# Weight lows split on chip in every pass of a Strassen layer, with reloads one tile at a time

## The chip, the cores and the metric

The kernel runs on one core of a Trainium2 chip. The metric is the device time of one execution in microseconds (us); lower is better. The engines are TensorE (PE in the profile, its weight loads PEld), VectorE (DVE), ScalarE (ACT), GpSimd (POOL) and SyncE (SP). DMAs are issued from SP's and POOL's queues here.

## The reference

One layer of a hybrid network is applied to a prompt of 2048 tokens and to a decoding batch of 64 tokens, model width 1024, all in float32. Cut to what matters (`B, T` are batch and tokens):

```python
h = rms_norm(x, g_pre)
vA, bA, cA, zA, q, f, iv, zB, gA, gB = split_cols(h @ w_in)     # w_in: 1024 x 10240
u = cA * vA
conv = causal_conv3(concat(conv_hist, u), conv_w)               # three taps
yA = (silu(zA) * bA * conv) @ w_a_out
fg = lb + (1 - lb) * sigmoid(f);  logf = log(fg);  kk = 1 - fg
S_new, o = hgrn2_scan(S0, silu(q) * QK_SCALE, kk, iv, logf)     # gated linear attention, 8 heads, chunks of 64
o = o * rsqrt(mean(o * o) + EPS) * g_onorm
yB = (o * silu(zB)) @ w_b_out
out = (sigmoid(gA) * yA + sigmoid(gB) * yB) @ w_o
x = x + rms_norm(out, g_post)
gate = sigmoid(rms_norm(x, g_ple) @ w_ple_gate)
x = x + (p @ w_ple_proj) * gate
```

The outputs are the new x of both token sets, the last two columns of u and the attention states.

## The kernel before

**Passes.** The 2112 tokens are cut into three blocks of 768, 704 and 640 columns (`SIZES`). Each block is one pass over all weights, so every weight is read from device memory three times. Activations lie with features on the partitions. A pass runs the gates gA and gB (`gates`), the heads (`path_b`: two weight groups a head, and the attention), path A (`path_a`), then the merges W_A, W_B and the output W_O, then two norms (`final_norm`) and the gate W_G. Work of neighbouring passes is interleaved: the norm of one pass runs as side work during the gates of the next, and `final_gate` of one pass runs at a later place.

**Precision.** A float32 operand x is split into hi, x rounded to the reduced format float32r (a cast on ScalarE), and lo = x - hi (a subtraction on VectorE). `split` (L195) is this pair. A product is hi·hi + hi·lo + lo·hi, three matmuls.

**Strassen.** Weights come in column pairs (i1, i2). With two halves of the contraction this makes four weight blocks of 128 x 4 x 128 numbers, 256 KB each: A11, A21, A22, A12. Seven products with A11, A12, A22 ("plain" blocks, taken as they are) and the sums S1 to S4 replace eight. One product of one pair is 4 x 3 = 12 matmuls. `sgroup` (L363) does the seven products of one pair in the order of `PRODUCTS`: A11, S3, S1, S2, A12, A22, S4. `combined` (L301) gives it the weights. A pass has 40 such pairs before its merges: 8 of the gates, 16 of the heads, 16 of path A. In the first pass two of them (the last of gB, and FF/QQ of head 0) are done by `plain_group` (L427) without Strassen.

`in_turn` (L486) does W_A, W_B and W_O, and W_G in the last pass, in another order: each of the seven products of `IN_TURN` (A11, A12, S2, S3, A22, S1, S4) for all four pairs, then the next. I call one of these seven a turn; it has four products, g = 0 to 3.

**Where hi and lo of weights come from.** In the first pass `combined` loads the four raw blocks, forms the sums on VectorE, splits all seven, and stores to device memory the sums (`keep_sum`, L288) and all seven lows (`split_w`, L221, stores when it is given a key that it has not seen). In later passes `kept_w` (L294) loads the raw block or the stored sum, casts hi on ScalarE, and *loads* the low: `split_w` finds the key in `lows`, takes a buffer from `low_tile` (L211) and issues the load on SP's queue. Such a group has 14 loads of 256 KB.

**Buffers.** `raw` has 5 tiles, `hi` 5, `lo` 4, and `s` (sums in the first pass) 3. `low_tile` counts its calls and gives an s tile at three of seven calls and a lo tile at the others. A DMA waits on its queue until the tile's last reader is done, and everything behind it on that queue waits too.

**Side work.** `hook()` is called after each product and runs the next piece of other work from a list written out by hand: steps of the attention (`head_attn`), of the norm, of the next pass's operands. `prepare_sums` (L327) computes sums S1 to S4 of W_A, W_B, W_O and W_G ahead of their use, in pieces. A piece is one sum on VectorE (L359), its split (L196), and two stores from POOL's queue (L341, L345); the raw blocks come by POOL as well (L336). In the first pass, the eight pairs of W_A and W_B are prepared during the heads, 4 pieces a head, and the four pairs of W_O during path A (`side`, L1384).

**Reloads.** Tensors spilled earlier come back through POOL's queue in the merge stage: gA tiles, attention outputs ("o") and gB tiles by `loads` (L1136), four tiles after certain turns; in the last pass the rows "h2" of the pass before, by `rows_again` (L1231), four tiles at a time and then four splits. `paced` (L253) makes such a DMA wait for the matmul issued last before it.

**Order.** The Tile framework places instructions by priority and keeps that order on each engine; `tc.high_priority()` moves weight loads, casts and splits forward, `issue_after` and `behind_all` queue side work behind named instructions.

Of the kernel before, what the change touches and what calls it, by code (L numbers as in the profile page):

```python
# [18 lines left out]
P = 128  # L19
D = 1024  # L20
KB = D // P
# [67 lines left out]
def hybrid_step(  # L89
# [31 lines left out]
    def nm(s):  # L121
        uid[0] += 1
        return f"{s}_{uid[0]}"
# [86 lines left out]

    def low_tile():  # L211

        turn[0] += 1
        if turn[0] % 7 in (1, 3, 5):
            return sum_tile(F32R)
        return wp.tile([P, 4, P], F32R, tag="lo", name=nm("lo"))
# [4 lines left out]
    def split_w(raw, key=None, queue=SP):  # L221

        hi = wp.tile([P, 4, P], F32R, tag="hi", name=nm("hi"), bufs=5)
        if key in lows:
            lo = low_tile()
            A.copy(hi, raw)  # L226
            SP.dma_start(lo.bitcast(F32), lows[key])
            return hi, lo
        lo = wp.tile([P, 4, P], F32R, tag="lo", name=nm("lo"))
        split(raw, hi, lo)  # L230
        if key is not None:
            lows[key] = dram.tile([P, 4, P], F32, tag=f"lo{key}", name=nm("low"), bufs=1)
            queue.dma_start(lows[key], lo.bitcast(F32))
        return hi, lo
# [59 lines left out]
    def kept_w(i1, i2, name, anew=False):  # L294

        keys = dict(A11=(i1, 0), A12=(i1, 1), A22=(i2, 1))
        if name in keys:
            return split_w(load_raw(w_blk[keys[name]]), None if anew else keys[name])
        return split_w(load_raw(sums[i1][name]), (i1, name))

    def combined(i1, i2, first):  # L301

        queue = SP if first else G
        with tc.high_priority():
            if not first and i1 in sums:
                return {n: kept_w(i1, i2, n) for _, n, _, _, _ in PRODUCTS}
            a11, a21, a22, a12 = (load_raw(w_blk[i, h]) for i, h in ((i1, 0), (i2, 0), (i2, 1), (i1, 1)))
            out = dict(A11=split_w(a11, (i1, 0), queue))
# [10 lines left out]
            out["A12"] = split_w(a12, (i1, 1), queue)  # L319
            out["A22"] = split_w(a22, (i2, 1), queue)  # L320
# [165 lines left out]
    def in_turn(stages, operand):  # L486
# [10 lines left out]
        for i, (st, n) in enumerate(todo):  # L497
# [44 lines left out]
            yield st["idx"], n  # L542
# [497 lines left out]
    def path_b(bl, hc, first, kept, fills, hs, extra, phases):  # L1040
# [13 lines left out]
        for hd in range(NH):  # L1054
# [6 lines left out]
            for i, before in enumerate((wait, 0, wait, 1)):  # L1061
                hooks.extend([None] * before)
                hooks.extend(partial(step_of, g, extra if i in phases else None) for g in attn)
                hooks.extend([None] * (NPART - len(attn)))
# [56 lines left out]
    def merge_in_turn(a, kept, mg):  # L1121
# [14 lines left out]
        def loads(idx, n):  # L1136
# [9 lines left out]
            if kind is not None:  # L1146
                tiles.extend(reload(kept[kind, j], n >= 0) for j in range(len(tiles), len(tiles) + KH))
# [6 lines left out]
    def out_in_turn(mg, xo, acc):  # L1154
# [14 lines left out]
        return dict(idx=W_O, raw=mg, sink=sink, anew=())  # L1169
# [61 lines left out]
    def rows_again(kept, h2):  # L1231

        for _ in range(2):
            for j in range(len(h2), len(h2) + KH):
                hi, lo = (rt(wide(kept["h2", j]), F32R) for _ in range(2))
                paced(G.dma_start(lo.bitcast(F32), kept["h2", j]))
                h2.append((hi, lo))
            yield
            for hi, lo in h2[-KH:]:
                split(lo.bitcast(F32), hi, lo)  # L1240
            yield
# [127 lines left out]
    for bi, bl in enumerate(blocks):  # L1369
# [4 lines left out]
        in_heads = pairs_of(W_A) + pairs_of(W_B) if first else late if middle else None  # L1374
        in_path = pairs_of(W_O) if first else pairs_of(W_G) if bl["last"] else None
# [8 lines left out]
        def side(rows, sums_):  # L1384
            for j in range(KB):
# [4 lines left out]
                elif sums_ is not None:  # L1390
                    at = (2, 9) if j < KB - 2 else (2, 6, 10)
# [10 lines left out]
        stages.append(out_in_turn(mg, xo, acc))  # L1402
# [10 lines left out]
        loads(W_A, -1)  # L1413
        for idx, n in in_turn(stages, a_first):
# [3 lines left out]
            if idx == W_O and n in (0, 2, 3, 5):  # L1418
                next(again)
            if (idx, n) == (W_O, 4):  # L1420
# [73 lines left out]
```

## Time and profile before

| | |
|---|---|
| median of three runs | 2576.79 us (2576.73 to 2579.15) |
| the profiled execution | 2578.22 us |
| its span, first to last instruction | 2576.4 us |
| granted PE clock, mean | 0.998 |
| PE busy | 2546.8 us (99%) |
| DVE, ACT busy | 1730.9 us (67%), 1589.4 us (62%) |
| DMA | 775.87 MB, 301 GB/s over the span |

Where the stages lie in the profile, from the timeline (start to end, us): first pass, start and plain groups to 78; gates, heads and path A 78 to 703; merges 704 to 887. Second pass, gates 887 to 986 and, after the first pass's W_G (986 to 1054), heads and path A 1054 to 1563; merges 1563 to 1728. Third pass, gates, heads and path A 1728 to 2284; merges 2284 to 2442, with W_O from about 2384; then W_G of the second pass to 2506 and of the third from 2521 to the end.

How to read it: one execution, recorded by the hardware. `L380` is line 380 of the kernel before. `lo<-low` is a load of a stored low into a lo tile, `s<-low` the same into an s tile, `low<-lo` a store; `pg` and `pa` are PSUM tiles of products and of the attention; `r` is a tile of the large ring buffer. A row of waits such as `PE pa L614 <- DVE r L634: 0.3, 1, 0.3` says that PE was idle before instructions of L614 that write a pa tile for 0.3 us in total, once, the longest 0.3, and that the VectorE instruction of L634 ended the wait. Ends of matmuls are modelled, so a busy PE need not be at its peak; the number of matmuls in a stretch without waits tells the pace.

### The profile page before, as it was taken

The numbers are of one execution on the slowest core, as the hardware profiler recorded it, in microseconds if no ns is written. First come the engines' busy times: TensorE is split into PE (matmuls) and PEld (weight loads), VectorE is DVE, ScalarE is ACT, GpSimd is POOL, SyncE is SP. The second block draws the span as 40 slices with busy tenths as digits, with TensorE's granted clock in tenths as the row PEclk, the third lists the DMA queues.
The fourth block names the chain that finished last, engine by engine and source line by source line (L and its number), as shares of the span: only waits on it lengthen the run. The fifth ranks groups of instructions, "written<-read, shape, count | busy, mean of one in ns | idle before, by whom it ended". The sixth has DMA issues, their size and how long they took to land. (4 is left out here: it accounts for less than half of the span.)

```text
span 2576.4 us, 47338 instructions
## 1 busy us (share of the span) xinstructions
PE 2546.8 (99%) x16246; PEld 2530.9 (98%) x16246; DVE 1730.9 (67%) x3378; ACT 1589.4 (62%) x3076; POOL 393.6 (15%) x718
## 2 busy tenths in 40 slices
PE   8999999999999999999999999999999999999999
PEld 8999999999999999999999999999999999999998
DVE  8788888889989855555554437974345554468766
ACT  6666676545555754577774546676677765566736
POOL 1122121221110011121011001102100011110221
PEclk9999999999999999999999999999999999999999
DMA  7889988999898898787778889989977789999977
GB/s 271 290 303 321 322 294 307 336 340 345 299 323 276 288 384 287 239 298 239 230 225 291 290 272 314 319 292 393 371 245 248 248 293 367 359 332 340 330 268 258
DMA packets 377553, 775.87 MB, mean 301 GB/s; under 512 B 46400, under 2 KB 51040, under 8 KB 377312
## 3 DMA queue, kind: packets, MB, share of 16 engines
q1 hardware_dynamic: 334368, 606.55, 69.7%
q0 software_dynamic: 42656, 166.25, 17.6%
q8 instruction: 128, 2.10, 0.3%
q14 instruction: 113, 0.93, 0.1%
q10 hardware_dynamic: 288, 0.05, 0.0%
HBM read 562.67 MB, written 209.99 MB: 300 GB/s over the span
## 5 line engine op out<-in xcount | busy, mean ns | idle before, releaser
L378 PE MATMUL pg<-r,hi 128*128 128x320 f32 (+2 forms) x3304 | 1086.1, 329 | 0.0
L379 PE MATMUL pg<-r,hi 128*128 128x320 f32 (+2 forms) x3304 | 1067.0, 323 | 0.0
L226 ACT CAST hi<-raw 128x512 fp32r<-128x512 f32 x780 | 480.0, 619 | 510.3 <-PE pg L379 204.5
L380 PE MATMUL pg<-r,lo 128*128 128x384 f32 (+2 forms) x2356 | 767.5, 326 | 3.4 <-DMA lo<-low 2.1
L378 PEld LDWEIGHTS pg<-r,hi 128*128 128x128 f32 x3304 | 621.6, 188 | 0.6 <-issue 0.2
L379 PEld LDWEIGHTS pg<-r,hi 128*128 128x128 f32 x3304 | 621.9, 188 | 0.0
L380 PEld LDWEIGHTS pg<-r,lo 128*128 128x128 f32 x2356 | 442.7, 188 | 4.9 <-DMA lo<-low 3.2
L513 PE MATMUL pg<-r,hi 128*128 128x320 f32 (+2 forms) x1120 | 360.9, 324 | 0.4 <-DVE r L196 0.2
L512 PE MATMUL pg<-r,hi 128*128 128x320 f32 (+2 forms) x1120 | 355.3, 325 | 2.1 <-ACT r L196 2.1
L380 PE MATMUL pg<-r,s 128*128 128x352 f32 (+1 forms) x948 | 299.9, 316 | 2.8 <-DMA s<-low 2.8
L196 DVE TENSOR_TENSOR r<-r,r 128x320 fp32r<-128x320 f32 (+7 forms) x394 | 230.3, 603 | 60.0 <-ACT r L196 58.7
L514 PE MATMUL pg<-r,lo 128*128 128x320 f32 (+2 forms) x756 | 243.9, 324 | 6.2 <-DMA lo<-low 6.2
L513 PEld LDWEIGHTS pg<-r,hi 128*128 128x128 f32 x1120 | 211.2, 189 | 4.2 <-DVE r L196 3.3
L512 PEld LDWEIGHTS pg<-r,hi 128*128 128x128 f32 x1120 | 209.4, 189 | 5.6 <-ACT r L196 5.3
L196 ACT CAST hi<-raw 128x512 fp32r<-128x512 f32 x206 | 127.4, 621 | 136.0 <-PE pg L379 47.3
L196 ACT CAST r<-r 128x320 fp32r<-128x320 f32 (+7 forms) x394 | 204.8, 552 | 9.9 <-DVE r L359 2.6
L380 PEld LDWEIGHTS pg<-r,s 128*128 128x128 f32 x948 | 178.0, 188 | 3.6 <-DMA s<-low 3.6
L403 DVE TENSOR_TENSOR hf<-hf,hf 128x352 f32<-128x352 f32 (+2 forms) x118 | 61.6, 522 | 166.9 <-ACT hf L392 166.1
L196 DVE TENSOR_TENSOR lo<-raw,hi 128x512 fp32r<-128x512 f32 x206 | 141.5, 689 | 44.7 <-PE pg L550 17.8
L196 ACT CAST hi<-s 128x512 fp32r<-128x512 f32 x160 | 98.8, 618 | 116.6 <-PE pg L379 94.7
L392 ACT COPY hf<-pg 128x352 f32<-128x352 f32 (+2 forms) x354 | 156.3, 445 | 7.4 <-PE pg L380 7.2
L514 PEld LDWEIGHTS pg<-r,lo 128*128 128x128 f32 x756 | 142.8, 189 | 7.1 <-DMA lo<-low 7.1
(367 smaller groups left out, 3907.9 us busy)
## 6 DMA issues: line engine op xcount, KB each, us to landing
raw<-w_blk SPq DMA_DIRECT2D x554, 256.0 KB, 4.2
raw<-S SPq DMA_DIRECT2D x472, 256.0 KB, 4.5
lo<-low SPq DMA_DIRECT2D x445, 256.0 KB, 4.4
s<-low SPq DMA_DIRECT2D x335, 256.0 KB, 4.4
low<-lo SPq DMA_DIRECT2D x308, 256.0 KB, 4.2
S<-s SPq DMA_DIRECT2D x152, 256.0 KB, 3.8
r<-w_blk POOLq DMA_DIRECT2D x72, 256.0 KB, 7.4
S<-r POOLq DMA_DIRECT2D x72, 256.0 KB, 4.9
```

The lines of the kernel that those rows point to most:

```text
L196: return A.copy(hi, src).ins, V.tensor_tensor(lo, src, hi.bitcast(F32), ALU.subtract).ins
L226: A.copy(hi, raw)
L378: add(hi[:, k, :], xhi, start=start and k == 0, stop=False)
L379: add(hi[:, k, :], xlo, start=False, stop=False)
L380: last[0] = add(lo[:, k, :], xhi, start=False, stop=k == KH - 1).ins
L392: copied = A.copy(got[n], ps[bank])
L403: adds[0] = V.tensor_tensor(got[1], got[1], got[2], ALU.add).ins
L512: add(hi[:, k, :], xhi, start=start and k == 0, stop=False)
L513: add(hi[:, k, :], xlo, start=False, stop=False)
L514: last[0] = add(lo[:, k, :], xhi, start=False, stop=k == KH - 1).ins
```

## The change

1. *Lows of plain blocks.* In the first pass `combined` splits A11, A12 and A22 without a key, so their lows are not stored. In later passes `kept_w` is called with `anew=True`: it loads the raw block and splits it, cast on ScalarE and subtraction on VectorE, into a lo tile. The lows of S3, S1 and S2 are loaded into the three s tiles, that of S4 into a lo tile. `plain_group` still stores its lows. W_O's plain blocks are split anew in the last pass only.
2. *Reloads.* `in_turn` now yields after each product and not after each turn. `loads` issues one tile after each product of the turns in which it issued four after the last. `rows_again` issues one tile after every second product of turns 1, 2, 4 and 5 of W_O (before: four after turn 1, four after turn 4) and splits one tile after each product of turns 3 and 6 (before: four after each).
3. *First head.* In the first pass head 0 runs no piece of `prepare_sums`. The last pair of W_B moves to path A, where `side` runs three pieces instead of two at j = 2 to 5.

The diff, cut to its core:

```diff
     def low_tile():
         turn[0] += 1
-        if turn[0] % 7 in (1, 3, 5):
-            return sum_tile(F32R)
-        return wp.tile([P, 4, P], F32R, tag="lo", name=nm("lo"))
+        return sum_tile(F32R) if turn[0] % 7 in (1, 3, 5) else lo_tile()
...
-    def split_w(raw, key=None, queue=SP):
+    def split_w(raw, key=None, queue=SP, low=low_tile):
...
         if key in lows:
-            lo = low_tile()
+            lo = low()
...
-    def kept_w(i1, i2, name, anew=False):
+    def kept_w(i1, i2, name, anew=False, low=low_tile):
         keys = dict(A11=(i1, 0), A12=(i1, 1), A22=(i2, 1))
         if name in keys:
             return split_w(load_raw(w_blk[keys[name]]), None if anew else keys[name])
-        return split_w(load_raw(sums[i1][name]), (i1, name))
+        return split_w(load_raw(sums[i1][name]), (i1, name), low=low)
...
             if not first and i1 in sums:
-                return {n: kept_w(i1, i2, n) for _, n, _, _, _ in PRODUCTS}
+                lows_in = dict(S3=partial(sum_tile, F32R), S1=partial(sum_tile, F32R), S2=partial(sum_tile, F32R), S4=lo_tile)
+                return {n: kept_w(i1, i2, n, True, lows_in.get(n)) for _, n, _, _, _ in PRODUCTS}
...
-            out = dict(A11=split_w(a11, (i1, 0), queue))
+            out = dict(A11=split_w(a11))
...
-            out["A12"] = split_w(a12, (i1, 1), queue)
-            out["A22"] = split_w(a22, (i2, 1), queue)
+            out["A12"] = split_w(a12)
+            out["A22"] = split_w(a22)
...
                 hook()
-            yield st["idx"], n
+                yield st["idx"], n, g
...
-                hooks.extend(partial(step_of, g, extra if i in phases else None) for g in attn)
+                hooks.extend(partial(step_of, g, extra if i in phases and (hd or not first) else None) for g in attn)
...
-        def loads(idx, n):
+        def loads(idx, n, count=1):
...
-                tiles.extend(reload(kept[kind, j], n >= 0) for j in range(len(tiles), len(tiles) + KH))
+                tiles.extend(reload(kept[kind, j], n >= 0) for j in range(len(tiles), len(tiles) + count))
...
-        return dict(idx=W_O, raw=mg, sink=sink, anew=())
+        return dict(idx=W_O, raw=mg, sink=sink, anew=anew)
...
     def rows_again(kept, h2):
-        for _ in range(2):
-            for j in range(len(h2), len(h2) + KH):
-                hi, lo = (rt(wide(kept["h2", j]), F32R) for _ in range(2))
-                paced(G.dma_start(lo.bitcast(F32), kept["h2", j]))
-                h2.append((hi, lo))
-            yield
-            for hi, lo in h2[-KH:]:
+        for o in (0, KH):
+            for j in range(o, o + KH):
+                h2.append(tuple(rt(wide(kept["h2", j]), F32R) for _ in range(2)))
+                paced(G.dma_start(h2[j][1].bitcast(F32), kept["h2", j]))
+                yield
+            for hi, lo in h2[o:]:
                 split(lo.bitcast(F32), hi, lo)
-            yield
+                yield
...
-        in_heads = pairs_of(W_A) + pairs_of(W_B) if first else late if middle else None
-        in_path = pairs_of(W_O) if first else pairs_of(W_G) if bl["last"] else None
+        in_heads = (pairs_of(W_A) + pairs_of(W_B))[:-1] if first else late if middle else None
+        in_path = pairs_of(W_B)[-1:] + pairs_of(W_O) if first else pairs_of(W_G) if bl["last"] else None
...
-                    at = (2, 9) if j < KB - 2 else (2, 6, 10)
+                    at = (2, 6, 10) if j > (1 if first else KB - 3) else (2, 9)
...
-        stages.append(out_in_turn(mg, xo, acc))
+        stages.append(out_in_turn(mg, xo, acc, ("A11", "A12", "A22") if bl["last"] else ()))
...
-        loads(W_A, -1)
-        for idx, n in in_turn(stages, a_first):
+        loads(W_A, -1, KH)
+        for idx, n, g in in_turn(stages, a_first):
             loads(idx, n)
...
-            if idx == W_O and n in (0, 2, 3, 5):
+            if idx == W_O and (n in (2, 5) or n in (0, 1, 3, 4) and g % 2 == 0):
                 next(again)
-            if (idx, n) == (W_O, 4):
+            if (idx, n, g) == (W_O, 4, KH - 1):
                 norms = [final_norm(bl, [s], xo, acc[0], h2, None, True) for s in segs]
```

More of the change, by code (lines that the diff above doesn't have):

```diff
@@ L209, in hybrid_step, with lo_tile @@
     lows, turn = {}, [0]
+    def lo_tile():
+        return wp.tile([P, 4, P], F32R, tag="lo", name=nm("lo"))
     def low_tile():
         turn[0] += 1
-        if turn[0] % 7 in (1, 3, 5):
-            return sum_tile(F32R)
-        return wp.tile([P, 4, P], F32R, tag="lo", name=nm("lo"))
+        return sum_tile(F32R) if turn[0] % 7 in (1, 3, 5) else lo_tile()
     def sum_tile(dt=F32):
         return wp.tile([P, 4, P], dt, tag="s", name=nm("s"), bufs=3)
-    def split_w(raw, key=None, queue=SP):
+    def split_w(raw, key=None, queue=SP, low=low_tile):
         hi = wp.tile([P, 4, P], F32R, tag="hi", name=nm("hi"), bufs=5)
         if key in lows:
-            lo = low_tile()
+            lo = low()
             A.copy(hi, raw)
@@ L228, in split_w @@
             return hi, lo
-        lo = wp.tile([P, 4, P], F32R, tag="lo", name=nm("lo"))
+        lo = lo_tile()
         split(raw, hi, lo)
@@ L1152, in merge_in_turn, with out_in_turn @@
         ], loads
-    def out_in_turn(mg, xo, acc):
+    def out_in_turn(mg, xo, acc, anew):
         xo.extend([None] * KB)
```

## The prediction, made before the change was run

> **What bounds the kernel now.** I read the page's shares first, then the list of what TensorE (PE) waited for, then busy time by stretch, and last the groups and DMA issues that the change touches.
>
> ```profile
> span 2576.4 us, 47338 instructions
> PE 2546.8 (99%) x16246; PEld 2530.9 (98%) x16246; DVE 1730.9 (67%) x3378; ACT 1589.4 (62%) x3076; POOL 393.6 (15%) x718
> ```
>
> PE is idle for 2576.4 - 2546.8 = 29.6 us, and the number of matmuls does not change, so only idle time and clock can move. The waits of PE (total, times, longest):
>
> ```profile
> PE pa L1093 <- ACT r L196: 6.9, 1, 6.9
> PE pg L514 <- DMA lo<-low: 6.2, 3, 3.9
> PE pg L380 <- DMA s<-low: 2.8, 3, 1.6
> PE pg L512 <- ACT r L196: 2.1, 3, 1.0
> PE pg L380 <- DMA lo<-low: 2.1, 3, 1.6
> PE pa L1035 <- DVE r L1030: 1.6, 1, 1.6
> PE pg L380 <- DVE lo L196: 1.3, 1, 1.3
> ```
>
> The 6.9 is the start of the kernel, which the change leaves alone. Three rows, 6.2 + 2.8 + 2.1 = 11.1 us in nine waits, are a low of a weight that was still on its way; two more, 1.6 and 1.3, are VectorE (DVE) being late. These 14.0 us in eleven waits are what the change aims at. Two things come on top. Stretches without a wait give PE's real pace, and the two longest waits leave a slower clock behind them (columns: PE, PEld, DVE, ACT and POOL busy, granted clock, DMA share, GB/s):
>
> ```profile
> 550.00:600.00 50.00, 48.73 (x278) 48.23 (x277) 44.01 (x81) 25.67 (x57) 13.79 (x23) 1.00 0.96 342
> 600.00:650.00 50.00, 50.00 (x287) 50.00 (x286) 45.45 (x75) 23.91 (x44) 8.24 (x14) 1.00 0.96 342
> 1750.00:1800.00 50.00, 48.11 (x324) 46.82 (x323) 28.02 (x45) 31.36 (x61) 10.75 (x18) 1.00 1.04 399
> 2150.00:2200.00 50.00, 50.00 (x342) 50.00 (x341) 23.49 (x41) 27.03 (x53) 7.14 (x16) 1.00 1.01 363
> ...
> 748.00:752.00 4.00, 2.92 (x9) 2.92 (x10) 1.53 (x4) 0.32 (x1) 0.00 (x0) 0.61 1.03 389
> 2424.00:2428.00 4.00, 0.28 (x2) 0.03 (x1) 2.29 (x6) 1.66 (x4) 0.00 (x0) 1.00 1.03 381
> 2428.00:2432.00 4.00, 3.85 (x16) 3.81 (x17) 0.08 (x1) 1.06 (x3) 0.00 (x0) 0.57 0.95 351
> ```
>
> 50 us / 287 is 0.174 us a matmul in the first pass, 50 / 342 is 0.146 in the last; a product of twelve takes 2.09 and 1.75 us. The profile's matmul is longer than its pace, since its end is modelled:
>
> ```profile
> L380 PE MATMUL pg<-r,lo 128*128 128x384 f32 x1064 | 358.7, 337 | 1.3 <-DVE lo L196 1.3
> ```
>
> So each wait costs 0.337 - 0.174 = 0.16 us more than its row: 11 x 0.16 = 1.8 us. The clock of 0.61 and 0.57 behind the two long waits costs 4 x 0.39 + 4 x 0.43 = 3.3 us. All that the change aims at is 14.0 + 1.8 + 3.3 = 19.1 us.
>
> **Lows made on chip.** Of the loads and stores of 256 KB, and of the copies and subtractions:
>
> ```profile
> lo<-low SPq DMA_DIRECT2D x445, 256.0 KB, 4.4
> s<-low SPq DMA_DIRECT2D x335, 256.0 KB, 4.4
> low<-lo SPq DMA_DIRECT2D x308, 256.0 KB, 4.2
> ...
> DMA packets 377553, 775.87 MB, mean 301 GB/s; under 512 B 46400, under 2 KB 51040, under 8 KB 377312
> ```
>
> ```profile
> L226 ACT CAST hi<-raw 128x512 fp32r<-128x512 f32 x780 | 480.0, 619 | 510.3 <-PE pg L379 204.5
> ...
> L196 DVE TENSOR_TENSOR lo<-raw,hi 128x512 fp32r<-128x512 f32 x206 | 141.5, 689 | 44.7 <-PE pg L550 17.8 <-PE pg L380 12.1 <-DMA low<-lo 6.8
> ```
>
> Three lows of each Strassen group go (A11, A12, A22; the six that the two plain groups of the first pass store stay, though nobody loads them now): 38 groups x 3 = 114 stores in the first pass; 114 loads and 2 x 3 more in the second; 40 x 3 and 4 x 3 of W_O in the last: 252 of the 780 loads, 114 of the 308 stores. That is 366 x 0.262 = 95.9 MB of 775.87. ScalarE casts as often as before. DVE gets 252 subtractions of 0.689, some 174 us.
>
> What this frees: the six waits of L380 for lows (4.9 us) lie, by the list of waits taken stretch by stretch, between 900 and 950 and between 1750 and 1850, where a pass's gates meet the norm of the pass before. There the DMA queues move 399 GB/s at a share of 1.04. A group of 84 matmuls lasts 84 x 0.146 = 12.3 us; three loads less are 0.786 MB / 12.3 us = 64 GB/s, which leaves 335. At 363 GB/s PE ran 50 us without a wait. I take all 4.9.
>
> The 1.3 us wait for a low from DVE in the first pass starts with a store:
>
> ```profile
> 572.50 0.69 DVE L196 TENSOR_TENSOR lo<-s,hi 128x512 fp32r<-128x512 f32 x1 [3.40 <-DMA low<-lo]
> ```
>
> DVE sat 3.40 us because the four lo buffers were still being stored. Three of a group's seven stores go, so three of seven lo tiles come free with their last matmul. I take the 1.3.
>
> What it costs: the new subtraction waits on DVE's queue for ScalarE's cast, which itself waits for a hi buffer (204.5 us for PE in its row). Queued behind it are the sinks that free PSUM banks and the attention's steps, and PE waits for both. The first pass is the nearest row: it makes 266 group lows on DVE, with DVE busy 44 to 45 of 50 us, at a price of one wait, 1.3 + 0.16. The third pass shows DVE at 23 to 28 of 50; three subtractions a group of 12.3 us add 17% to that. 252 / 266 of 1.46 is 1.4 us: that is my value. (In the last W_O twelve of them fall among the operands of the next turn; the L512 row shows what a late operand costs, 0.7 each time.) It cannot be below nothing, as a freed load is counted above; the upper end is the slower rival. With the S lows in the three s tiles and the rest in the four lo tiles, each buffer still comes back after seven products, so a load keeps a lead of 12 us against a landing of 4.4: nothing.
>
> **Reloads one tile a product.** Rows of the timeline for the two longest waits, with what POOL issued before them (start, us, engine, line; in brackets the idle time before it and what ended it), and one row of the chain that ended last (start, us, what):
>
> ```profile
> 738.73 0.54 POOL L1116 DMA_DIRECT2D r<-o  x1 [14.95 <-ACT hi L226]
> 739.50 1.59 POOL L1116 DMA_DIRECT2D r<-o  x3 [0.24 <-issue]
> 741.09 1.06 POOL L638 DMA_DIRECT2D r<-x_fm  x2
> ...
> 749.08 0.69 PE L514 MATMUL pg<-r,lo 128*128 128x384 f32 x1 [2.13 <-DMA lo<-low]
> ...
> 2415.15 0.54 POOL L1236 DMA_DIRECT2D r<-h  x1 [19.42 <-PE pg L514]
> 2416.24 1.59 POOL L1236 DMA_DIRECT2D r<-h  x3 [0.55 <-issue]
> 2417.82 1.59 POOL L1183 DMA_DIRECT2D r<-x_fm  x3
> ...
> 2428.15 0.57 PE L514 MATMUL pg<-r,lo 128*128 128x320 f32 x1 [3.87 <-DMA lo<-low]
> ```
>
> ```profile
> 2417.55 10.55 DMA lo<-low
> ```
>
> In the last W_O, four tiles of 352 KB and three of 160 leave within 4 us, and a low issued among them lands after 10.55 us instead of 4.4. In the first W_A it is four of 384 KB and two of 352. A turn below is one of the seven products done for four column pairs, so four products of twelve matmuls. With the change the h tiles go out behind every second product of W_O's first two and of its fourth and fifth turns. In the fourth, weights and h ask (2 x 256 + 176) KB / 1.75 us = 403 GB/s and, since A22's low is no longer loaded, in the fifth (256 + 176) KB / 1.75 = 253. The three x_fm tiles still come together. I take both waits and the 0.2 beside them (6.2) and the 3.3 of the clock. The eight splits of the h tiles stay eight, now one a product. POOL now waits for a matmul at each product instead of once in four; behind it stand only later loads of the same stage, and it sat 19.42 us there already: nothing.
>
> By the Trainium skill's page "TensorE: Matmul & The Clock Gate" (Part 1, the HAM clock gate), the clock halves after an idle window of about 3.4 us. Of this, the 3.87 us wait agrees, and the 2.13 us wait at 749 does not; by that rule the slow clock behind it would have another cause, which is a rival below.
>
> **First head without pieces.** The wait of 1.6 at L1035 ends with the last of these rows:
>
> ```profile
> 133.37 0.69 DVE L196 TENSOR_TENSOR r<-r,r 128x512 fp32r<-128x512 f32 x1
> 134.99 0.69 DVE L1030 TENSOR_TENSOR r<-pa,ms 128x512 f32<-128x512 f32 x1 [0.93 <-POOL ms L574]
> 136.99 0.68 DVE L359 TENSOR_TENSOR r<-r,r 128x512 f32<-128x512 f32 x1
> ...
> 139.52 0.42 DVE L1030 TENSOR_TENSOR r<-pa,ms 128x256 f32<-128x256 f32 x1
> ```
>
> DVE has no idle time between them but 0.93 us. The piece's subtraction and the next piece's sum take two places of 0.6 us ahead of L1030, and two earlier pieces another 2.4 us of a DVE that is behind. I take the 1.6. The four pieces move into the first path A, 4 x 1.2 us of DVE where it is busy 44 to 45 of 50: a third of one wait, 0.5 us; at most one wait more, 1.5, at least nothing.
>
> **Sum.** 4.9 + 1.3 + 6.2 + 1.6 = 14.0, with 1.8 and 3.3: 19.1 gained; 1.4 + 0.5 paid; 17.2 us net. The profiled execution took 2578.22 us, its span 2576.4; it would take 2561.0. It lies 1.4 above the median of 2576.79, so the median goes to 2559.6. If nothing is paid and the L512 waits (2.1 + 3 x 0.16), which follow a reload burst too, go as well: 2555. Some smaller gaps below a row's limit put the low end at 2552. With twice the price and one long wait left (2.1 + 0.16 + 1.6) it is 2565.
>
> **The rivals.**
> *The bursts only spread.* In the first pass, weights and one 384 KB tile a product ask 896 KB / 2.09 us = 439 GB/s, over the 399 of the busiest stretch, in W_A's fourth, sixth and seventh turns. Then both long waits stay: 6.0 + 0.3 + 3.3 = 9.6 us, 2569. Against it: loads run some products ahead, and the W_O numbers above.
> *Slower: DVE's queue becomes the releaser.* In 80 groups of passes two and three the first low, A11's, now stands in DVE's queue behind a blocked cast. A wait like that at 573 costs 1.46; 13 of them eat 19.1, 17 make it slower by 0.2%; in every third group, 27 x 1.46 = 39 us, 2597. For it: 204.5 us of casts waiting for PE. Against it: the first pass.
> *Slower: POOL's powers held up.* The pow of each norm takes very unequal time, and the attention waits for it:
>
> ```profile
> L574 POOL TENSOR_TENSOR ms<-ms,mhalf x56: 537/1002/1737, 133.5 to 2103.0; 128x4 f32<-128x4 f32 x24, 128x1 f32<-128x1 f32 x16, 128x2 f32<-128x2 f32 x8, 64x1 f32<-64x1 f32 x8
> ...
> 1915.85 0.29 DVE L1030 TENSOR_TENSOR one<-pa,ms 128x128 f32<-128x128 f32 x1 [0.67 <-POOL ms L574]
> ...
> 1918.67 0.27 PE L1035 MATMUL pa<-ident,one 128*128 128x128 f32 x1
> ```
>
> If each added subtraction that meets a pow delays it by its own 0.69, the 2.5 us between L1030's end and L1035 take almost four such delays to use up; at one wait of 0.69 in each of the 40 parts of the later passes it would be 28 us, 2587. The Trainium skill's page "SBUF — State Buffer" (Who interferes with whom) states the cause: a VectorE operation on two SBUF inputs and a GpSimd operation that reads SBUF lock each other out. The unequal 537 to 1737 ns fit it.
> *The slow clock at 749 has another cause.* Its wait is barely half as long as the one at 2428, and the stretch from 1750 to 1800, idle for 1.9 us in several waits, kept 1.00. Then 1.6 of the 3.3 us stays: 2561.
> *Hidden anyway.* Behind each late low another thing is nearly as late, the cast or the raw tile, and the new order of buffers brings waits of its own: 2 us remain of the gain, 2575.
>
> **The numbers.** The forecast 0.56 (2552 to 2566); the slow clock at 749 left, 0.10; bursts 0.14; hidden anyway 0.10; DVE's queue 0.07; powers 0.03. Measurement tells 0.2%, 5.2 us: faster is below 2571.6, slower above 2581.9. Faster: 0.56 + 0.10 + 0.10 of the bursts = 0.76. Same: 0.04 + 0.10 = 0.14. Slower: 0.10. The range 2552 to 2575 holds nearly all of the first three and half of the fourth, 0.8.
>
> **What would show it.** Right: no row of L380 for a low; L514's below 0.5 us; no L1035 row; a clock of 1.00 around 750 and 2430; some 680 MB; DVE busy near 1905 us; 1750 to 1800 near 335 GB/s with PE at 50.00. Wrong: PE rows that name lo from L196 in later passes, sinks or L1035 waiting for DVE or POOL, or L514 still waiting for lows right after reloads.

## The result and the profile after

| | before | after |
|---|---|---|
| median of 17 runs each | 2578.96 us (2574.83 to 2582.54) | 2573.2 us (2567.89 to 2579.5) |
| the profiled execution | 2578.22 us | 2570.03 us |
| its granted PE clock | 0.998 | 0.999 |

The ratio is 0.9979 [0.9971, 0.9986]: the change gains 5.8 us of the 17.2 forecast. Single runs of one kernel differ by up to 12 us, so the tables below go by medians of several runs. The profiled execution of the kernel after lies 3.2 us under its median.

The medians below leave out four executions that took far longer than the rest: one each of dve_twice, dve_twice_raw6 and reload_head_raw6, at a granted clock of 0.85, 0.87 and 0.75, and one of the kernel before that took 9754 us.

The shares and the DMA total, from the page of the kernel after:

```profile
span 2567.7 us, 47073 instructions
PE 2543.4 (99%) x16246; PEld 2528.9 (98%) x16246; DVE 1886.0 (73%) x3630; ACT 1591.9 (62%) x3076; POOL 391.0 (15%) x718
...
DMA packets 324847, 679.89 MB, mean 265 GB/s; under 512 B 40544, under 2 KB 45184, under 8 KB 324608
...
L196 DVE TENSOR_TENSOR lo<-raw,hi 128x512 fp32r<-128x512 f32 x458 | 315.4, 690 | 168.2 <-ACT hi L196 127.2
```

The traffic fell by 95.98 MB as worked out, and 252 subtractions more stand in DVE's group. The work moved as planned; the waits did not go. What PE waited for after the change (in `after.py` the matmuls of `sgroup` are L380 to L382, of `in_turn` L514 to L516; the third of each uses the low):

```profile
PE pa L1095 <- ACT r L196: 6.9, 1, 6.9
PE pg L516 <- DMA lo<-low: 5.0, 4, 2.5
PE pg L382 <- DMA s<-low: 3.4, 2, 2.2
PE pg L382 <- DMA lo<-low: 1.2, 1, 1.2
PE pg L514 <- ACT r L196: 1.1, 1, 1.1
PE pg L515 <- DVE r L196: 0.8, 2, 0.7
```

L1035 and the wait for a low from DVE are gone. The groups' waits for lows are 3.4 + 1.2 = 4.6 us in three waits, after 4.9 in six, but they are other waits. Those of before stood between 923 and 927 and between 1754 and 1831 us, in later groups of the gates; none of the six is left. The three new ones stand at 886, 1730 and 1744, where a pass takes over from the one before (its gates begin at 882.4 and 1727.4). Of the waits of `in_turn` 5.0 of 6.2 are left. Stretches of the kernel after, the places shown of before (the end of W_O now lies some 9 us earlier) and two more (columns as in the prediction):

```profile
744.00:748.00 4.00, 3.02 (x17) 3.02 (x18) 0.08 (x1) 1.11 (x3) 0.54 (x1) 1.00 0.95 349
748.00:752.00 4.00, 4.00 (x25) 4.00 (x24) 3.93 (x8) 2.65 (x7) 1.07 (x2) 1.00 1.00 363
...
884.00:888.00 4.00, 1.84 (x11) 1.54 (x10) 3.97 (x7) 1.98 (x3) 0.00 (x0) 0.94 1.00 377
888.00:892.00 4.00, 4.00 (x18) 4.00 (x17) 0.18 (x1) 0.00 (x0) 0.00 (x0) 0.63 0.09 34
1750.00:1800.00 50.00, 50.00 (x346) 49.98 (x345) 35.92 (x57) 32.37 (x62) 11.28 (x19) 1.00 0.98 357
2416.00:2420.00 4.00, 3.31 (x22) 3.05 (x22) 3.16 (x8) 3.19 (x9) 2.12 (x4) 1.00 1.02 365
2420.00:2424.00 4.00, 4.00 (x30) 4.00 (x29) 3.11 (x7) 3.22 (x7) 0.00 (x0) 1.00 1.03 397
```

1750 to 1800 came out as forecast, PE runs through; at the end of W_O a wait of 0.7 us is left and the clock stays at 1.00. The loss is new at 886: there PE waits and then has a clock of 0.63, and the DMA share falls to 0.09 just behind. The same stretch of the kernel before:

```profile
884.00:888.00 4.00, 4.00 (x25) 4.00 (x24) 4.00 (x10) 2.77 (x6) 1.20 (x3) 1.00 0.94 311
888.00:892.00 4.00, 4.00 (x27) 4.00 (x26) 3.71 (x6) 1.98 (x4) 0.00 (x0) 1.00 0.97 360
```

From the first matmul of each stage to the first of the next, in the traces (before, then after): first gates, heads and path A 625.7 and 621.9 us; the boundary stage that begins at 887 with the second gates 99.5 and 101.2; the second heads and path A 509.6 and 509.8; the second merges 165.1 and 166.4; the third gates, heads and path A 555.5 and 553.7; the third merges 158.7 and 153.0. The rest differs by 0.6 or less. So 3.8 + 1.8 + 5.7 us came in and 1.7 + 1.3 were given back.

### The profile page after: what moved, and what is told of

It is laid out like the page before. It is cut to its first block, busy times and chain, and to the rows that moved or that the text cites. A ratio compares the mean times of both kernels' runs of the same rounds, so it can differ in the third digit from the quotient of the medians.

```text
span 2567.7 us, 47073 instructions
## 1 busy us (share of the span) xinstructions
PE 2543.4 (99%) x16246; PEld 2528.9 (98%) x16246; DVE 1886.0 (73%) x3630; ACT 1591.9 (62%) x3076; POOL 391.0 (15%) x718
## 5 line engine op out<-in xcount | busy, mean ns | idle before, releaser
L380 PE MATMUL pg<-r,hi 128*128 128x320 f32 (+2 forms) x3304 | 1088.6, 329 | 0.0
L382 PE MATMUL pg<-r,lo 128*128 128x384 f32 (+2 forms) x2368 | 772.0, 326 | 1.2 <-DMA lo<-low 1.2
L380 PEld LDWEIGHTS pg<-r,hi 128*128 128x128 f32 x3304 | 622.6, 188 | 0.4
L382 PEld LDWEIGHTS pg<-r,lo 128*128 128x128 f32 x2368 | 445.4, 188 | 1.6 <-DMA lo<-low 1.4
L196 DVE TENSOR_TENSOR lo<-raw,hi 128x512 fp32r<-128x512 f32 x458 | 315.4, 690 | 168.2 <-ACT hi L196 127.2
L515 PE MATMUL pg<-r,hi 128*128 128x320 f32 (+2 forms) x1120 | 360.8, 324 | 1.1 <-DVE r L196 0.8
L514 PE MATMUL pg<-r,hi 128*128 128x320 f32 (+2 forms) x1120 | 354.5, 324 | 1.1 <-ACT r L196 1.1
L382 PE MATMUL pg<-r,s 128*128 128x320 f32 (+1 forms) x936 | 296.6, 317 | 3.4 <-DMA s<-low 3.4
L516 PE MATMUL pg<-r,lo 128*128 128x320 f32 (+2 forms) x776 | 249.8, 323 | 5.0 <-DMA lo<-low 5.0
L515 PEld LDWEIGHTS pg<-r,hi 128*128 128x128 f32 x1120 | 210.6, 188 | 5.0 <-DVE r L196 4.2
L514 PEld LDWEIGHTS pg<-r,hi 128*128 128x128 f32 x1120 | 208.4, 188 | 4.9 <-ACT r L196 4.5
L382 PEld LDWEIGHTS pg<-r,s 128*128 128x128 f32 x936 | 176.8, 189 | 4.0 <-DMA s<-low 4.0
L516 PEld LDWEIGHTS pg<-r,lo 128*128 128x128 f32 x776 | 145.8, 188 | 6.3 <-DMA lo<-low 6.2
L196 DVE TENSOR_TENSOR lo<-s,hi 128x512 fp32r<-128x512 f32 x160 | 110.3, 689 | 36.7 <-PE pg L382 12.8
```

The lines of the kernel that those rows point to most:

```text
L196: return A.copy(hi, src).ins, V.tensor_tensor(lo, src, hi.bitcast(F32), ALU.subtract).ins
L380: add(hi[:, k, :], xhi, start=start and k == 0, stop=False)
L382: last[0] = add(lo[:, k, :], xhi, start=False, stop=k == KH - 1).ins
L514: add(hi[:, k, :], xhi, start=start and k == 0, stop=False)
L515: add(hi[:, k, :], xlo, start=False, stop=False)
L516: last[0] = add(lo[:, k, :], xhi, start=False, stop=k == KH - 1).ins
```

## Where the new wait comes from

SP's issues of lows ahead of 886 and the wait itself, from the timeline of the kernel after:

```profile
872.18 0.32 SPq L228 DMA_DIRECT2D s<-low  x1
...
876.35 0.33 SPq L228 DMA_DIRECT2D s<-low  x1
...
880.53 0.34 SPq L228 DMA_DIRECT2D s<-low  x1
...
886.53 0.43 PE L382 MATMUL pg<-r,s 128*128 128x352 f32 x1 [2.16 <-DMA s<-low]
```

The same issues in the kernel before, whose gates begin at 886.7 and not at 882.4:

```profile
874.31 0.32 SPq L227 DMA_DIRECT2D lo<-low  x1
876.40 0.32 SPq L227 DMA_DIRECT2D s<-low  x1
878.49 0.32 SPq L227 DMA_DIRECT2D lo<-low  x1
880.60 0.32 SPq L227 DMA_DIRECT2D s<-low  x1
```

The first group of the gates takes over the buffers of W_O, whose turns still hand out lo and s tiles in the old rotation: a tile comes free with every product, 2.1 us apart, but an s tile only with every second one. Before, the group's lows followed that rotation, and those of A11, S3, S1 and S2 were issued every 2.1 us. After, S3, S1 and S2 all want s tiles, and their issues are 4.2 us apart. This group takes its first four products interleaved, so it needs all four lows at once: in the kernel before S2's is issued 886.7 - 880.6 = 6.1 us ahead of the gates' first matmul, in the kernel after 882.4 - 880.5 = 1.9 us. PE went on 886.5 - 880.5 = 6.0 us after the issue, when that low had landed. For the same reason the three s tiles come back only when all four products are done, and what stands behind the next group's first s tile on SP's queue is late too. The waits of SP's queue of the kernel after, from 860 to 895:

```profile
SPq L228 <- PE pg L382: 8.6, 1, 8.6
...
SPq L206 <- DVE lo L196: 4.8, 2, 2.4
```

For 8.6 us the queue stands before the next group's first s tile, and the DMA share falls to 0.09 (before, the longest stand there was 5.2). At the handover from the second pass to the third the three s lows are issued at 1716.0, 1721.8 and 1725.7, and the gates begin at 1727.4: PE waits at 1730. S4's low of this group is issued at 1739.5, behind the three s lows of the next group, and PE waits again at 1744.

A second hold shows in the whole lists for SP's queue, of the kernel before and of the kernel after:

```profile
SPq L206 <- DVE lo L196: 200.7, 155, 17.2
```

```profile
SPq L206 <- DVE lo L196: 536.7, 364, 17.2
```

L206 loads a raw tile. In `kept_w` before, ScalarE's cast was the last reader of a raw tile; for the plain blocks it is now DVE's subtraction. There are five raw tiles, and 364 waits end with DVE in place of 155. The row says where the queue stands; whether PE loses anything by it, it does not say.

My theory was then: the gain is there, but two holds give it back, (1) the first group's lows in s tiles, (2) raw tiles kept by DVE. The rivals: the three parts hinder each other; DVE's queue is the price; the freed traffic is worth nothing.

## The experiments

All are medians, with the ratio to the kernel before run alongside and its 95% interval (before took 2578.09, 2576.89, 2578.35 and 2578.44 us in the four sets; times of different sets can be laid side by side no closer than these differ).

| kernel | us | ratio to before |
|---|---|---|
| lows_only | 2581.68 | 1.0010 [1.0000, 1.0019] |
| reload_only | 2571.29 | 0.9974 [0.9964, 0.9985] |
| head_only | 2574.47 | 0.9989 [0.9980, 0.9997] |
| changed_again | 2573.32 | 0.9984 [0.9975, 0.9993] |
| first_group_tiles | 2567.46 | 0.9961 [0.9949, 0.9974] |
| merge_a22_split | 2574.76 | 0.9986 [0.9977, 0.9995] |
| tiles_and_a22 | 2568.96 | 0.9967 [0.9955, 0.9980] |
| dve_twice | 2580.4 | 1.0015 [1.0005, 1.0024] |
| reload_and_head | 2570.59 | 0.9974 [0.9962, 0.9985] |
| tiles_raw6 | 2563.30 | 0.9943 [0.9931, 0.9955] |
| changed_raw6 | 2570.89 | 0.9970 [0.9960, 0.9981] |
| reload_head_raw6 | 2570.30 | 0.9975 [0.9965, 0.9985] |
| dve_twice_raw6 | 2570.60 | 0.9972 [0.9961, 0.9983] |
| all_mended_a22 | 2564.15 | 0.9948 [0.9934, 0.9962] |

**The three parts alone, and the whole again.** Each of the first three is the kernel before with one part of the change, whose first lines are these:

```diff
 # lows_only
-                return {n: kept_w(i1, i2, n) for _, n, _, _, _ in PRODUCTS}
+                return {n: kept_w(i1, i2, n, True, lows_in.get(n)) for _, n, _, _, _ in PRODUCTS}
 # reload_only
-            yield st["idx"], n
+                yield st["idx"], n, g
 # head_only
-        in_heads = pairs_of(W_A) + pairs_of(W_B) if first else late if middle else None
+        in_heads = (pairs_of(W_A) + pairs_of(W_B))[:-1] if first else late if middle else None
```

> The first of the three parts alone (lows of plain blocks made on chip, lows of S3, S1, S2 in the s tiles), reloads and first head as before. The theory of the prediction: the waits for lows in the gates go and nothing takes their place, 4.9 + 1.3 us with their 0.16 each, less 1.4 paid, some 6 us faster. The theory formed on the changed kernel's trace (tiles): the gates' old waits go, but the first group of the second and of the third pass waits for a low of S, 2 us and 1.3 us, and the third pass again for S4's low; the net of this part is then below 3 us. Both: the wait of 1.6 us for L1030 in head 0 stays.

> The second part alone (one tile a product), lows loaded and stored as before. The theory of the prediction: both long waits of the merges go, 6.2 us with 3.3 us of clock, some 10 us faster. The rival (the demand of the turn, not the burst): only the wait in the last W_O shrinks, from 3.9 us, and the one in the sixth turn of the first W_A stays at 2 us or more; some 5 us faster.

> The third part alone (head 0 without pieces, four pieces more in path A). The theory of the prediction: the 1.6 us wait of L1035 goes, and the 1.3 us wait for a low in path A stays, as it starts with stores: 1.8 us faster at most. A rival (DVE is full in path A): further waits for lows from DVE appear in path A, and the time does not fall.

> The changed kernel once more, for a second profile beside the first. If the waits of the first profile belong to the program, the same ones are there: at the start of the second and third passes, in the sixth turn of the first W_A, 8 to 10 us in all besides the start. If they are luck, they lie elsewhere. What may differ is whether the clock halves behind them.

Against 2578.09 the parts alone give +3.6, -6.8 and -3.6 us, together -6.8; the whole gives -4.8. Reloads and first head run together (reload_and_head, below) give -7.8 where they give -10.4 alone. By the spread of the runs the parts may simply add up, but that they hinder each other by 2 or 3 us is not excluded. The part that was to bring most, the lows, brings nothing: by its interval it costs between 0 and 5 us. Its waits:

```profile
PE pg L516 <- DMA lo<-low: 8.7, 3, 4.4
...
PE pg L382 <- DMA s<-low: 3.9, 2, 3.0
PE pg L514 <- ACT r L196: 2.9, 1, 2.9
PE pg L382 <- DMA lo<-low: 2.0, 1, 2.0
```

The lows that PE waits for in L382 total 5.9 us, more than the 4.9 of before, and L514 waits 2.9 us for a cast early in the third W_A. In reload_only, where lows are loaded as before, these rows are smaller and the wait of 3.9 us in W_O is gone:

```profile
PE pg L514 <- DMA lo<-low: 4.0, 4, 2.5
PE pg L380 <- DMA s<-low: 2.6, 2, 1.9
PE pg L380 <- DMA lo<-low: 1.6, 3, 0.9
```

**The first group's tiles.** The changed kernel, with the old rotation for the lows of the first group of a pass:

```diff
-                lows_in = dict(S3=partial(sum_tile, F32R), ...
+                lows_in = {} if i1 == GA * 8 else dict(S3=partial(sum_tile, F32R), ...
-                return {n: kept_w(i1, i2, n, True, lows_in.get(n)) ...
+                return {n: kept_w(i1, i2, n, True, lows_in.get(n, low_tile)) ...
```

> The changed kernel, with one group of each later pass changed: the first group of the gates takes its four S lows from the old rotation of s and lo tiles instead of S3, S1, S2 from the three s tiles. If the s tiles are what delays the first group (they are handed on by the last turns of W_O and, inside the group, given back only after four products), the waits of 2.2, 1.3 and 1.2 us at the start of the second and third passes go, with the slow clock behind the first: 4 to 7 us faster than the changed kernel. If the cause is that raw tiles are now held until DVE has subtracted, so that SP's queue runs late, they stay.

It is 5.9 us faster than the change (2573.32), and all waits of L382 are gone. What PE still waited for in it, beside the start:

```profile
PE pg L516 <- DMA lo<-low: 4.3, 4, 3.1
PE pg L514 <- ACT r L196: 2.1, 1, 2.1
PE pg L515 <- DVE r L196: 1.5, 3, 0.7
```

This shows hold (1): an edit of two lines, which changes no work and no traffic, takes the L382 rows away. (It also moves the rotation of the merges behind it on by four tiles a pass, so the other waits need not stay the same.)

**A22 of W_A and W_B split anew.** By the count of matmuls from the first of W_A, the wait near 745 is at the first product of its sixth turn, so for a low of S1. For the turn before, that of A22, the first pass stores four lows. This removes these stores, and the loads of A22's lows in the later passes:

```diff
-            dict(idx=W_A, raw=a, sink=sink_a, anew=("A11", "A12")),
-            dict(idx=W_B, raw=ob, sink=sink_b, anew=("A11", "A12")),
+            dict(idx=W_A, raw=a, sink=sink_a, anew=("A11", "A12", "A22")),
+            dict(idx=W_B, raw=ob, sink=sink_b, anew=("A11", "A12", "A22")),
```

> The changed kernel, with A22's low of W_A and W_B split on chip in every pass too (four stores and eight loads less in each merge). If the wait in the sixth turn of the first W_A comes from what the turn before asks of the DMA queues (raw tiles, stores of A22's lows, reloads, x), the 2.5 us there go: 2.5 to 4 us faster than the changed kernel. If it comes from the reloads alone, it stays.

> Both edits together. If each wait has its own cause the gains add: 6 to 10 us faster than the changed kernel, near 2565.

Nothing gained: 2574.8 against 2573.3, and with the first edit 2569.0 against 2567.5. The wait fell to 0.8 and 1.6 us and the first merges from 183.3 to 181.2, but the third pass's gates, heads and path A took 558.0 in place of the 553.7 and 556.2 of the change's two profiles. The waits of L382 at its start account for that: 3.2 + 1.3 + 0.4 us and 1.7 of a half clock behind the first, for 1.3 + 1.2 and 3.2 + 1.7 in the change's profiles. Without them the three took 551.4, 551.3 and 551.3 us. Why a handover is hit harder in one profile than in another, I have not found.

**Without the lows, and a sixth raw tile.** The first is the kernel before with the parts on reloads and the first head. The second is first_group_tiles with one raw tile more, paid with one of the four buffers of a small tile (cut; the other place that takes a raw tile gets `bufs=6` too):

```diff
-        raw = wp.tile([P, 4, P], F32, tag="raw", name=nm("raw"), bufs=5)
+        raw = wp.tile([P, 4, P], F32, tag="raw", name=nm("raw"), bufs=6)
-        qc = small.tile([P, 2, MAXN // CH], F32, tag="qc", name=nm("qc"))
+        qc = small.tile([P, 2, MAXN // CH], F32, tag="qc", name=nm("qc"), bufs=3)
```

> The second and third parts together, with all lows stored and loaded as before. If the lows made on chip cost as much at the first groups of the passes as they save elsewhere, this is 3 to 6 us faster than the whole change, near 2568. If the lows are worth the 6 us of the prediction, it is slower than the whole change by some us.

> The changed kernel with the first groups on the old rotation of tiles, and a sixth raw tile (one buffer of qc less, to make room). A raw tile is now held until DVE has subtracted. If that delays SP's queue and with it the first products of the merges (waits for narrowed operands of 1.1 to 2.9 us near 2290 and of 0.5 to 0.7 near 1570, which only the kernels with lows on chip show in that size), these go, some 2 to 4 us faster than the same kernel with five. If not, no difference.

reload_and_head is at 2570.6, so in the changed kernel the lows on chip cost 2573.3 - 2570.6 = 2.7 us. tiles_raw6 is the fastest kernel here: 4.2 us under first_group_tiles, no run of the one as slow as the fastest of the other, 15 us under before. Its waits beside the start:

```profile
PE pg L516 <- DMA lo<-low: 3.8, 2, 2.6
PE pg L382 <- DMA lo<-low: 0.8, 1, 0.8
```

The rows of L514 and L515 for late casts and splits, 2.1 + 1.5 us in first_group_tiles, are gone too. How such a wait came about shows in first_group_tiles, early in the third W_A:

```profile
2286.95 0.62 ACT L227 CAST hi<-raw 128x512 fp32r<-128x512 f32 x1 [2.58 <-DMA raw<-S]
...
2288.15 0.46 ACT L196 CAST r<-hf 128x320 fp32r<-128x320 f32 x1
...
2288.30 0.90 PE L514 MATMUL pg<-r,hi 128*128 128x320 f32 x2 [2.10 <-ACT r L196]
```

ScalarE stood 2.58 us for a late raw tile, the cast of PE's operand stood behind it, and PE waited 2.10 us for that cast. With six raw tiles ScalarE waits for no raw tile there. The queue's own row hardly moved, though; in tiles_raw6 it is

```profile
SPq L206 <- DVE lo L196: 519.2, 363, 5.5
```

So the 537 us of the kernel after are not the price of the hold; most of them delay nothing that PE needs. The price is read from what the sixth tile gains.

**Whose raw tile.** The same sixth tile in the changed kernel with nothing else, and in reload_and_head, which has no new subtraction:

> The changed kernel with a sixth raw tile (qc from four buffers to three) and nothing else; the rotation of the first group's lows stays as in the changed kernel. Theory A, raw tiles held by VectorE's subtraction: the sixth tile gives back about what it gave beside the old rotation, 4.2 us, so 2569 against 2573.3, and the waits of L382 for s lows near 888 and 1730 stay. Theory B, a sixth raw tile gives any kernel more lead: the same 2569. Theory C, the sixth tile pays only once the first group's rotation is mended: 2573, no change.

> Reloads and first head only, lows loaded as in the kernel before, with a sixth raw tile. Theory A: without the new subtractions a raw tile is given back by ScalarE's cast and a sixth changes little: 2570, within 1.5 us of the 2570.6 without it. Theory B: 2566, as much gain as beside the lows on chip; then the lows on chip are worth only 3 us or so once all is mended.

Without the lows it does nothing (2570.3 and 2570.6). In the changed kernel it gains 2.4 us, and the handover gets worse: one wait of the s lows at 890.99 is now

```profile
890.99 0.66 PE L382 MATMUL pg<-r,s 128*128 128x352 f32 x1 [4.35 <-DMA s<-low]
```

So the sixth tile mends a thing that came with the lows. That this thing is the raw tile kept by the subtraction is the likely reading, not shown by itself: no run gave the raw tile back earlier and left the rest as it was. With both holds mended the lows on chip gain 2570.3 - 2563.3 = 7.0 us.

**Every new subtraction twice.** In later passes of the changed kernel, then of tiles_raw6, 234 subtractions are repeated with the same result (cut to the added lines):

```diff
         split(raw, hi, lo)
+        if low is None:
+            V.tensor_tensor(lo, raw, hi.bitcast(F32), ALU.subtract)
```

> The changed kernel, each new subtraction of the second and third passes done twice (234 more of 0.69 us on DVE, same result). If DVE's work has room, as the prediction priced it (1.4 us for 252), the time rises by 0 to 2 us. If DVE's queue is a releaser of PE, as in the slower rival, PE waits for lows from L196 appear in the later passes and the time rises by 5 us or more.

> A second profile of the kernel that makes each new subtraction of the later passes twice; it took some 7 us more than the changed kernel. If DVE's queue becomes a releaser in the steady groups, the heads and path A of the second pass (509.8 us in every profile so far) get longer. If DVE matters only where it is full, at the first groups and in the merges, they stay and the time is there.

> First group's old rotation, sixth raw tile, and each new subtraction of the later passes done twice (234 more, 161 us of VectorE). It does no other work, only more of it. With five raw tiles the doubling cost 7.5 us. Theory A, the cost of a subtraction is that it keeps the raw tile: with a sixth tile it costs less than half, at most 3.5 us: 2564 to 2567. Rival, the cost is VectorE's queue itself, sinks and attention steps late: 7.5 us again, 2571.

dve_twice_look is the same kernel as dve_twice, one execution of 2579.93 us with its profile. In it the second pass's heads and path A take 511.9 us (509.8 in the change), the third pass's gates, heads and path A 561.0 (553.7 and 556.2). With five raw tiles the doubling costs 2580.4 - 2573.3 = 7.1 us, with six 2570.6 - 2563.3 = 7.3. So here my theory that a subtraction's price is its hold on the raw tile fell, in the form in which I put it: a sixth tile does not halve it. What PE waited for in dve_twice_raw6:

```profile
PE pg L518 <- DMA lo<-low: 4.9, 2, 2.5
PE pg L384 <- DMA s<-low: 4.3, 2, 2.7
```

And two stretches of it, where the norm of the pass before runs beside the second group, then the same of tiles_raw6:

```profile
890.00:910.00 20.00, 17.98 (x115) 17.38 (x114) 13.85 (x24) 12.28 (x24) 4.29 (x6) 1.00 0.85 282
1735.00:1760.00 25.00, 21.40 (x137) 20.86 (x136) 15.91 (x28) 14.30 (x28) 5.33 (x8) 0.93 0.79 259
```

```profile
890.00:910.00 20.00, 19.88 (x128) 19.54 (x127) 11.85 (x20) 13.19 (x25) 4.28 (x6) 1.00 0.80 274
1735.00:1760.00 25.00, 25.00 (x173) 24.87 (x172) 16.78 (x29) 17.33 (x32) 8.00 (x13) 1.00 1.00 357
```

PE waits for lows while the DMA share is only 0.79: they were issued late, not carried slowly. DVE is busy 14 of 20 and 16 of 25 us, by no means full, so it is not the amount of its work that counts but when it comes. SP's raw loads that waited for a subtraction between 885 and 910, in dve_twice_raw6 and in tiles_raw6:

```profile
SPq L206 <- DVE lo L233: 6.2, 3, 3.6
```

```profile
SPq L206 <- DVE lo L196: 3.1, 2, 2.1
```

There the norm's wide steps and the doubled subtractions stand in one queue and SP's loads wait behind both. Between 1735 and 1760 this row is only 0.9 us; what made the lows late there is open. Elsewhere the doubling is nearly free: the second pass's heads and path A take 512.8 in place of 510.9 us. How much of this price the first, single subtractions pay is not measured; doubling only shows that DVE's queue has room for little more.

**All together.** tiles_raw6 with A22 split anew in W_A and W_B:

> First group's old rotation, sixth raw tile, and A22 of W_A and W_B split anew too. If the wait in W_A near 745 (2 to 3 us with its slow clock) goes and costs nothing later: 2561 against 2563.3. If, as with five raw tiles, the gain in the first W_A is lost in the third pass: 2563 to 2565. The last W_O and the half clock behind chance waits spread single runs by 2 us.

2564.15 against 2563.30: again nothing. The wait in W_A is 1.1 us, but a wait of L382 for a low, 3.5 us, stands near 1740 instead, at the other handover. I leave A22 as it is.

## Why the prediction was wrong, step by step

**The step that failed** is the sentence on buffers: "With the S lows in the three s tiles and the rest in the four lo tiles, each buffer still comes back after seven products [...]: nothing." It holds from one steady group to the next. It does not hold for the first group after W_O, which gets its tiles from turns that rotate in another way. New waits of 4.6 us and a half clock stand there, in place of the six that are gone. This step cost 5.9 us (first_group_tiles). The same paragraph named what stands behind the new subtraction on DVE's queue, and left out who waits for its operand to be given back: SP, with the raw tile. What a sixth raw tile mends is 4.2 us more (tiles_raw6; 2.4 where the first hold stands). 5.9 + 4.2 = 10.1 of the 11.4 us missing. The mended kernel, with one raw tile more than the prediction had, gains 15 us over before, near the 17.2.

**4.9 for the waits of L380: right for these waits.** All six are gone; the stretch at 1750 runs through with 357 GB/s where I put 335. The 4.6 us of the change are new waits, and with both holds mended 0.8 us is left. "Hidden anyway", with its "new order of buffers brings waits of its own", is the rival that comes nearest, at a chance of 0.10 and 2575; measured 2573.2. But only its second half came true. Its first half, another thing nearly as late behind each late low, did not, so that its time fits is in part luck.

**1.3 for the low from DVE and 1.6 for L1035: right.** Both rows are gone and the first gates, heads and path A are 3.8 us shorter. But the wait for DVE's low is no longer in the list of head_only either, and in reload_only, which leaves the first pass's groups as they were, it is 0.3 us. So the stores are not its only remedy, and part of the 1.3 was chance.

**6.2 and 3.3 for the reloads: right for W_O, wrong for W_A.** At the end of W_O the wait went from 3.87 (at 2428) to 0.69 (at 2419), the clock is 1.00, and the third merges are 5.7 us shorter. In W_A the wait stayed, 2.5 us for 2.1: the rival "the bursts only spread" holds in that one place. The pace of one tile a product is enough in W_O and not in W_A. The tiles of W_A are larger, 384 KB, and four lows of A22 are stored for the turn before; without these stores (merge_a22_split, tiles_and_a22, all_mended_a22) 0.8 to 1.6 us are left, in all other kernels it is 1.8 or more. The part on reloads brought 6.8 us alone where its terms are 6.2 + 0.5 + 3.3 = 10.0. The clock gave back less than 3.3: in the profile after, the slow stretch is at 888 and not near 750, in the second profile of the same kernel it is at both.

**1.4 for the subtractions: too small, by how much is open.** It was sized by how often PE waited in the first pass, which makes the same subtractions before and after. With the new first head that pass's gates, heads and path A take 621.6 to 622.3 us in each kernel, with the lows on chip or without, so its one wait was no price of a subtraction. In the steady second pass the new subtractions cost nothing (509.6 and 509.8). Doubled, those of the later passes cost 7.1 to 7.3, most of it in the third pass's gates, heads and path A (556.6 us for 550.3 in tiles_raw6) and little in the steady second pass. So the price of the second ones is not one wait in so many subtractions; it is paid at the handovers, where DVE has the norm to do as well.

**0.5 for the four pieces in path A: not settled.** head_only gained 3.6 where its terms give 1.6 + 0.16 - 0.5 = 1.3, the wait for DVE's low included in what it removes. Beside the reloads (reload_and_head against reload_only) the same part gains only 0.7, and its own interval reaches from 0.8 to 5.2.

**The rivals.** POOL's powers were not held up. The row after the change, to be laid beside the one in the prediction:

```profile
L576 POOL TENSOR_TENSOR ms<-ms,mhalf x56: 536/1003/1736, 131.2 to 2101.1; 128x4 f32<-128x4 f32 x24, 128x1 f32<-128x1 f32 x16, 128x2 f32<-128x2 f32 x8, 64x1 f32<-64x1 f32 x8
```

536, 1003 and 1736 ns for 537, 1002 and 1737, with 252 subtractions of two operands more on DVE: no delay by them can be seen. In the timeline of the kernel after none of them overlaps one of these powers. The unequal times, read as a sign of the delay, are mostly a matter of shape: one column takes 0.54 to 0.57 us, four columns 1.03. The longest, 1.60 to 1.74 us, are three powers of four columns with a VectorE operation on two SBUF tiles beside them (L821 of `after.py`), and they stand in both kernels. The slower rival, DVE's queue, was not decided by one wait in every third group, but it was closer than its 0.07 says: doubling the subtractions makes the kernel slower than before (1.0015). That the slow clock at 749 might have another cause than its wait is taken up at the end.

## What to carry to other kernels

When an operation takes over an operand from another, ask when the operand's buffer comes free, who is queued in order for it, and what happens at the seam between two loops that hand out the same buffers by different rules; a count that holds within a loop says nothing there. Look for the place in the waits of the DMA queue: its row went from 200.7 to 536.7 us, while PE's list only showed a late low. But do not take that row for the price: with a sixth tile 4.2 us were gained and the row stayed at 519.2. And test the parts of a change one by one before judging it: here one part of three cost 3 us, and with two lines and one tile it gained 7.

## What the runs showed of the hardware

The slow clock behind a wait does not follow from the wait's length as I had it. In the kernel after, the wait of 2.53 us at 745 left the clock at 1.00 (its two stretches are above). Behind that of 2.16 us at 886 the clock was 0.94 and 0.63 in two stretches of 4 us, which is 4 x 0.06 + 4 x 0.37 = 1.7 us lost. In tiles_raw6 the wait of 2.6 us at 746 did slow it:

```profile
744.00:748.00 4.00, 2.01 (x7) 2.02 (x8) 0.22 (x1) 0.00 (x0) 0.00 (x0) 0.78 1.05 391
748.00:752.00 4.00, 4.00 (x20) 4.00 (x19) 1.85 (x4) 1.85 (x4) 0.59 (x2) 0.79 0.58 183
```

4 x 0.22 + 4 x 0.21 is 1.7 us again. The Trainium skill's page "TensorE: Matmul & The Clock Gate" (Part 1, the HAM clock gate) has the clock halve after an idle window of about 3.4 us and lets the window run free of the kernel's work; the second half agrees with waits of one length having either effect, the first does not agree with 2.16 us. Over the traces of this case (all but that of dve_twice), no wait of 1.0 to 1.75 us had a half clock behind it, 20 of the 29 waits from 1.8 to 3.3 us had, and all seven of 3.5 us and more, the start left out. The half clock lasted 3.41 us or twice that. So a wait of 1.8 us or more costs itself and, by chance, 1.7 or 3.4 us on top. This explains part of the spread of single runs: of the 17 runs after, the fastest (2567.89 us) had a mean granted clock of 1.000 and the slowest (2579.5) of 0.997, which is 0.003 x 2573 = 7.7 us of the 11.6 between them.
